# A hybrid attention and SSD layer: query and key rows permuted for their stores, decay rows in one load

## The chip, the cores and the metric

The kernel runs on one core of one Trainium2 chip. A core has TensorE (PE in the profile: matmuls; PEld: its weight loads), VectorE (DVE), ScalarE (ACT), GpSimd (POOL) and SyncE (SP), and 16 DMA engines that move data between its on-chip memory and DRAM. Nearly all transfers are issued by SP, one after the other. The metric is device time in microseconds, and a kernel is told by the median of its runs.

## The reference

One layer over 1024 tokens of width 2048. One input projection gives everything: queries (8 heads of 128), keys and values (2 heads), a gate, the queries and the key of a small indexer, and the inputs of an SSD (state space) mixer with 16 heads of 64.

- **Attention.** The indexer scores all keys of a query's own and earlier chunks of 64; each query keeps the best 256 and attends to these alone. Queries and keys are rotated by position in the first 32 of their 128 dimensions, where dimension i < 16 is paired with i + 16:

```python
x1 = t32[..., :half]
x2 = t32[..., half:rot]
out = jnp.concatenate([x1 * cos - x2 * sin, x2 * cos + x1 * sin, t32[..., rot:]], axis=-1)
```

- **SSD.** A causal convolution, then in chunks of 64 a masked product with decays exp(a_l - a_s), where a is the running sum of dt * A of each head, and a state that is carried from chunk to chunk.
- Both outputs are gated, multiplied by one output projection, added to the scaled input and normalised.

A score is a sum over the 128 dimensions of a head, so it is the same in whatever order queries and keys hold these dimensions, as long as it is one order for both.

## The kernel before

**Numbers.** A float32 factor is split into a rounded high part (ACT, `wh`, `xh`) and the rest (DVE or POOL, `wl`, `xl`), and each product is three matmuls. The projections use a seven-product scheme for pairs of tiles, with sums of inputs (`xf`), sums of weights (`ts`) and saved products (`p`, `u`) that go out to DRAM and come back.

**Tiling.** The tokens are two halves of 512. A tile of the input projection is 128 columns of its matrix by 512 tokens, with the columns on the partitions; which columns, `tile_cols` says. Results collect in four PSUM tiles `pj`; scores, transposes and SSD products use `a` and `o`.

**Queries and keys.** A query tile j of a group of four holds, for each of the four heads, dimensions 32j to 32j + 31. So tile 0 holds all that is rotated, and only there `rope_rows` runs: a shuffle of partitions inside groups of 32 (`SW16`), two products with tables (`rq`, `rk`) and a sum. A key tile holds 64 dimensions of both heads, and again tile 0 is the rotated one. Each tile is then stored to scratch in DRAM, `q_sc` (heads, 128 dimensions, 512 tokens) or `k_sc`, as 4 heads x 32 rows or 2 heads x 64 rows of 2 KB. There are 16 query stores and 4 key stores. Attention loads them again as 128 dimensions of a head (`t_kv`, `t_attn`) after all of a group are there.

**Decay rows.** `t_dt` stores the running sums of a half as 64 rows of 128 in `arow`. An SSD unit `t_ssd(h, g)` runs two rounds (`cp`) of two chunks; each round loads its 2 x 4 rows to all 128 partitions (`ar`), by one load for each chunk, and then takes ACT through two exponentials (`ea`), eight ReLUs with the column of each head and one wide exponential. There are 16 rounds.

**What sets the order.** The kernel's text is a planner. `Sim` holds a clock for each engine and estimated costs; tasks are generators that yield what they need; `Flow.pump` takes the first task by priority that is ready by these clocks, and every engine gets its instructions in the order in which they were emitted. PE's own work list is fixed, and other tasks are put between. A DMA is priced by

```python
        issue = 1000.0 if eng == "G" else 350.0
        row = max(sb.ap[-1][1] * 4, 64)
        self.clk["D"] = x + max(out.size(), in_.size()) * 4 * (1 / 360 + 0.6 / row)
```

where `row` is the last dimension of the tile on the chip's side, and takes one of eight lanes (semaphores), each of which is free again when its transfer has landed. On the chip each engine runs its list in order, and an instruction waits for the semaphores of what it uses. Nearly every instruction is recorded under line 312 in the profile (the planner's call), so instructions are told apart by their tiles.

Of the kernel before, what the change touches and what calls it, by code (L numbers as in the profile page):

```python
# [18 lines left out]
P = 128  # L19
# [18 lines left out]
O_Q, O_K, O_V, O_Z = 0, 1024, 1280, 1536  # L38
# [32 lines left out]
def xbc_col(g, j):  # L71
    return (256 * g + 128 * j) if j < 2 else (1024 + 128 * g if j == 2 else 1536 + 128 * g)


def tile_cols(kind, j):
    if kind == "misc":
        return [(O_KI, 64), (O_WI, 16), (O_DT, 16)]
    if kind == "q":
        return [(O_Q + 128 * (j // 4 * 4 + r) + 32 * (j % 4), 32) for r in range(4)]
    if kind == "k":  # L80
        return [(O_K + 128 * g + 64 * j, 64) for g in range(2)]
    base = {"qi": O_QI, "v": O_V, "z": O_Z}
    if kind in base:
        return [(base[kind] + 128 * j, 128)]
    g, i = j
    if kind == "zs":
        return [(O_ZS + 256 * g + 128 * i, 128)]
    return [(O_X + xbc_col(g, i), 128)]
# [494 lines left out]
class Layer:  # L583
# [774 lines left out]
    def rope_rows(self, h, x, name):  # L1358

        fl = self.fl  # L1360
        yield Need("", us=3)
        cos, sin, tmp = [fl.new("us", [P, HALF]) for _ in range(3)]
        fl.dma(cos, self.a[name][0, :, h * HALF:(h + 1) * HALF])
        fl.dma(sin, self.a[name][1, :, h * HALF:(h + 1) * HALF])
        yield Need("V")
        yield from self.rope(x, x, tmp, cos, sin, self.SW16)
        fl.free(cos, sin, tmp)

    def table(self, name, h):
# [5 lines left out]
            self.tab[name, h] = t  # L1375
        return self.tab[name, h]

    SW16 = [(i ^ 16) for i in range(32)]
    SW8 = [(i ^ 8) if i < 16 else i for i in range(32)]

    def rope(self, x, ps, tmp, cos, sin, perm):
# [263 lines left out]
    def s_k(self, h, j, x):  # L1645
        fl = self.fl
        if j == 0:
            yield from self.rope_rows(h, x, "rk")
        yield Need()
        fl.dma(self.k_sc[h].rearrange("(g p) s -> g p s", g=2)[:, 64 * j:64 * j + 64], x)  # L1650
        fl.free(x)
        fl.signal(self.ev_kv[h, j, "k"])

# [8 lines left out]
    def s_q(self, h, n, x):  # L1662
        fl = self.fl
        if n % 4 == 0:
            yield from self.rope_rows(h, x, "rq")
        yield Need()
        t = n % 4
        fl.dma(self.q_sc[h][n // 4][:, 32 * t:32 * t + 32], x)
        fl.free(x)
        fl.signal(self.ev_q[h, n])  # L1670

# [292 lines left out]
    def t_ssd(self, h, g):  # L1964
        fl, nc = self.fl, self.nc
# [7 lines left out]
        for cp in range(2):  # L1973
# [9 lines left out]
            ar = fl.new("s4", [P, 2, 4, P])  # L1983
            bn, xdt, xdd, hs, ea = [fl.new("u", [P, 2, 256]) for _ in range(5)]
            ea = ea.rearrange("p a (b l) -> p a b l", b=2)
            rows = self.arow[h].rearrange("(c n) l -> c n l", c=4)[2 * cp:2 * cp + 2, 4 * g:4 * g + 4, :]
            for k in range(2):
                fl.dma(ar[:, k], rows[k].partition_broadcast(P))
            for k, c in enumerate(cs):
                yield Need("P", late=2500.0, a=1)  # L1990
                b = fl.new("a", [P, 512])
# [18 lines left out]
            for q in range(2):  # L2010
                rq = slice(64 * q, 64 * q + 64)
# [39 lines left out]
            for j in range(2):  # L2051
                yield Need("P", now=True)
                for k, c in enumerate(cs):
                    for hh in range(2):
                        r = 2 * j + hh
# [248 lines left out]
        yield from self.ln_apply(0, st, dc)  # L2304


def rope_table(rot, dim, rows):
    half = rot // 2
    inv = (THETA ** (-np.arange(half) * 2.0 / rot)).astype(np.float32)
    ang = (np.arange(S, dtype=np.float32)[None, :] * inv[:, None]).astype(np.float64)  # L2310
    cos, sin = np.ones((rows, S)), np.zeros((rows, S))
    for p in range(rows):
        j = p % dim
        if j < rot:
            cos[p] = np.cos(ang[j % half])
            sin[p] = np.sin(ang[j % half]) * (-1.0 if j < half else 1.0)
    return np.stack([cos, sin]).astype(np.float32)


def layout(x, w_in, w_out, conv_w, conv_b, dt_bias, a_log, d_skip, ssd_norm_w, ln_g, ln_b):  # L2320
    xn = x[0]
    xt = np.ascontiguousarray(xn.T.reshape(KT // 2, 2, P, 2, HALF).transpose(3, 0, 2, 1, 4))
    wt = np.zeros((len(ORDER), D, P), np.float32)
    for t, (kind, j) in enumerate(ORDER):
        c0 = 0
        for off, n in tile_cols(kind, j):
            wt[t, :, c0:c0 + n] = w_in[0][:, off:off + n]
            c0 += n
    wt = np.ascontiguousarray(wt.reshape(len(ORDER), 2, 8, P, P).transpose(0, 1, 3, 2, 4)).reshape(len(ORDER), 2, P, 1024)
    wo = w_out[0].reshape(KT, P, 4, 512)[E_ORDER].reshape(8, 2, P, 4, 512)  # L2330
    wo = np.ascontiguousarray(wo.transpose(3, 0, 2, 1, 4)).reshape(4, 8, P, 1024)
    cw = np.zeros((P, 16, 5), np.float32)
    for g in range(4):
        for j in range(4):
            c = xbc_col(g, j)
            cw[:, 4 * g + j, 0:4] = conv_w[0][:, c:c + P].T
            cw[:, 4 * g + j, 4] = conv_b[0][c:c + P]
    dn = np.stack([np.repeat(d_skip[0], 64).reshape(8, P).T, ssd_norm_w[0].reshape(8, P).T], axis=1)
    hp = np.stack([dt_bias[0], a_log[0]])
    c3 = np.stack([np.eye(P), np.triu(np.ones((P, P))), np.ones((P, P))], axis=1).astype(np.float32)  # L2340
    return dict(xn=xn, xt=xt, wt=wt, wo=wo, cw=cw, dn=np.ascontiguousarray(dn), hp=hp, c3=c3, ri=rope_table(16, 64, P),
                rq=rope_table(32, 32, P), rk=rope_table(32, 64, P), lng=ln_g[0], lnb=ln_b[0])


# [12 lines left out]
```

## Time and profile before

| | |
|---|---|
| median of 3 runs | 1665.69 us (1662.65 to 1666.38) |
| span of the profiled execution | 1666.1 us, its own time, 0.4 above the median |
| instructions | 23979 |
| mean granted TensorE clock | 0.992 of full |
| DMA | 414.48 MB in 192387 packets, 249 GB/s, 71.7% of 16 engines on SP's queue |

A line of a view of groups gives the line, the engine, the operation, the written tile, an arrow and the tiles read, shapes and a count. In a timeline a line begins with its start and its length in us, and ends with the idle time of the engine ahead of it and what released it. Matmuls overlap: one of 512 columns is drawn as 0.39 us long, and the next begins 0.23 us after it. The table of windows has a line for each stretch: its length, the busy time of each engine, the granted clock (PEclk), the busy share of the DMA engines and what they moved.

### The profile page before, as it was taken

Reading aid. Unit: us, or ns where it says so; the run is one execution under the profiler, and the core shown is the slowest. Engines: PE = TensorE matmul, PEld = TensorE weight load, DVE = VectorE, ACT = ScalarE, POOL = GpSimd, SP = SyncE. Lnnn points to the kernel's source line nnn. Section 1 sums busy time; section 2 is a strip of 40 time slices with the busy share of each in tenths; the row PEclk is TensorE's granted clock in tenths of the full one; section 3 lists DMA queues with packets and bytes.
Section 4 is the critical chain, followed back from the end, with each engine's and each line's share of the span. In section 5 each row is a group of like instructions: output and inputs, shape, how many; then the busy total and the mean of one; then the engine's idle time right before and its main releaser. Section 6 shows DMA issues by size and latency. Waiting matters only on the chain. (4 is left out here: it accounts for less than half of the span.)

```text
span 1666.1 us, 23979 instructions
## 1 busy us (share of the span) xinstructions
PE 1620.1 (97%) x7996; PEld 1340.9 (80%) x7996; DVE 1321.7 (79%) x2429; ACT 1002.0 (60%) x1770; POOL 197.3 (12%) x215
## 2 busy tenths in 40 slices
PE   9999999999998989999999999999999999999997
PEld 7787777888787768888888888888877888888885
DVE  5889998997778866788676669875787687659998
ACT  4555666779787788776344456776866555532330
POOL 0100010000000000122212202222010000100110
PEclk9999999999999999999999999999999999999999
DMA  8177574789768856687786584656988889668664
GB/s 309 52 280 258 189 262 168 268 303 334 290 230 324 294 196 234 235 304 277 260 288 218 180 286 161 210 171 210 334 284 307 316 300 325 215 232 274 220 202 152
DMA packets 192387, 414.48 MB, mean 249 GB/s; under 512 B 19720, under 2 KB 55688, under 8 KB 192264
## 3 DMA queue, kind: packets, MB, share of 16 engines
q1 hardware_dynamic: 191832, 412.56, 71.7%
q8 instruction: 63, 1.03, 0.2%
q14 instruction: 60, 0.49, 0.1%
q10 hardware_dynamic: 432, 0.39, 0.1%
HBM read 308.94 MB, written 103.94 MB: 248 GB/s over the span
## 5 line engine op out<-in xcount | busy, mean ns | idle before, releaser
L312 PE MATMUL pj<-xh,wh 128*128 128x512 f32 (+1 forms) x1496 | 585.7, 392 | 14.5 <-ACT u L312 6.0
L312 PE MATMUL pj<-xh,wl 128*128 128x512 f32 (+1 forms) x1496 | 573.6, 383 | 5.1 <-DVE wl L312 5.1
L312 PE MATMUL pj<-xl,wh 128*128 128x512 f32 (+1 forms) x1496 | 573.0, 383 | 0.0
L312 DVE TENSOR_TENSOR wl<-wr,wh 128x1024 fp32r<-128x1024 f32 (+2 forms) x236 | 282.4, 1201 | 172.4 <-ACT wh L312 170.4
L312 PEld LDWEIGHTS pj<-xh,wh 128*128 128x128 f32 x1496 | 283.8, 190 | 68.6 <-issue 7.5
L312 PEld LDWEIGHTS pj<-xh,wl 128*128 128x128 f32 x1496 | 283.5, 190 | 63.1 <-DVE wl L312 7.3
L312 PEld LDWEIGHTS pj<-xl,wh 128*128 128x128 f32 x1496 | 284.0, 190 | 49.1
L312 ACT ACTIVATE wh<-wr 128x1024 fp32r<-128x1024 f32 (+2 forms) x242 | 248.1, 1031 | 120.0 <-PE pj L312 82.8
L312 PE MATMUL a<-u,u 128*128 128x512 f32 (+3 forms) x736 | 172.8, 354 | 7.6 <-DVE s L312 4.4
L312 PEld LDWEIGHTS a<-u,u 128*128 128x128 f32 x736 | 120.7, 189 | 42.5 <-DVE s L312 18.6
L312 ACT ACTIVATE u<-a 128x512 fp32r<-128x512 f32 (+4 forms) x115 | 53.2, 479 | 153.3 <-DVE u L312 58.0
L312 ACT ACTIVATE u<-s,sm 128x640 bf16<-128x640 int16 (+7 forms) x132 | 129.7, 983 | 22.1 <-DVE sm L312 20.0
L312 DVE TENSOR_TENSOR u<-u,u 128x512 f32<-128x512 f32 (+6 forms) x204 | 128.6, 645 | 5.7 <-DMA u<-wo 1.3
L312 PE MATMUL pj<-wh,xh 128*128 128x512 f32 x310 | 125.2, 404 | 0.5 <-DVE u L312 0.5
L312 PE MATMUL pj<-wh,xl 128*128 128x512 f32 x310 | 121.0, 390 | 0.0
L312 PE MATMUL pj<-wl,xh 128*128 128x512 f32 x310 | 121.0, 390 | 0.0
L312 ACT ACTIVATE a<-a 128x512 f32<-128x512 f32 (+3 forms) x160 | 77.1, 505 | 68.3 <-PE a L312 65.5
L312 ACT ACTIVATE u<-u 128x512 f32<-128x512 f32 (+4 forms) x146 | 80.1, 558 | 52.4 <-DVE u L312 43.9
L312 DVE TENSOR_TENSOR u<-pj,u 128x512 f32<-128x512 f32 (+2 forms) x112 | 74.7, 668 | 45.7 <-PE pj L312 42.2
L312 DVE TENSOR_TENSOR wr<-wr,wr 128x1024 f32<-128x1024 f32 (+1 forms) x81 | 99.8, 1233 | 0.8 <-DMA wr<-wt 0.4
L312 POOL TENSOR_SCALAR s<-s,sm 128x640 f32<-128x640 f32 (+7 forms) x64 | 63.8, 1011 | 124.0 <-DVE sm L312 97.4
L312 DVE SCALAR_TENSOR_TENSOR u<-cv,cw,u 128x512 f32<-128x512 f32 x96 | 73.0, 766 | 6.7 <-ACT u L312 3.5
(259 smaller groups left out, 2200.3 us busy)
## 6 DMA issues: line engine op xcount, KB each, us to landing
wr<-wt SPq DMA_DIRECT2D x187, 512.0 KB
u<-u SPq DMA_DIRECT2D x110, 256.0 KB
wr<-t SPq DMA_DIRECT2D x44, 512.0 KB
u<-wo SPq DMA_DIRECT2D x64, 256.0 KB
ts<-u SPq DMA_DIRECT2D x64, 256.0 KB
wr<-ts SPq DMA_DIRECT2D x32, 512.0 KB
s<-xt SPq DMA_DIRECT2D x24, 512.0 KB
t<-wr SPq DMA_DIRECT2D x22, 512.0 KB
```

The source lines that it names most:

```text
L312: f(*args, **kw)
```

## The change

The 128 dimensions of a head get a new order, `head_dim`. Row 4i + t of a query head is held in tile t at place i, so the four tiles of a group take every fourth row; a key tile takes every second. Rows 0, 4, 8 ... (tile 0) are still the 32 rotated dimensions, now with the pairs i and i + 16 next to each other, so that the shuffle swaps neighbours (`SW1` for queries; for keys, where the same rows lie two apart, `SW2`). The columns of the matrix are laid out on the host in that order, and the tables too. A tile's 4 heads x 32 rows are then rows t, t + 4, t + 8 ... of a scratch of 512 rows: one dimension of 128 rows, 8 KB apart (4 KB for keys). The bytes, the row length of 2 KB, the shuffles, products and loads stay as they are.

Each round of an SSD unit loads its decay rows by one DMA of 128 x 2 x 512 floats in place of two of 128 x 4 x 128.

```diff
+def head_dim(row):
+    i, t = divmod(row, 4)
+    return 32 * t + i if t else i // 2 + 16 * (i % 2)
+
 def tile_cols(kind, j):
...
     if kind == "q":
-        return [(O_Q + 128 * (j // 4 * 4 + r) + 32 * (j % 4), 32) for r in range(4)]
+        return [(O_Q + 128 * (j // 4 * 4 + r) + head_dim(4 * i + j % 4), 1) for r in range(4) for i in range(32)]
     if kind == "k":
-        return [(O_K + 128 * g + 64 * j, 64) for g in range(2)]
+        return [(O_K + 128 * g + head_dim(2 * i + j), 1) for g in range(2) for i in range(64)]
...
-        yield from self.rope(x, x, tmp, cos, sin, self.SW16)
+        yield from self.rope(x, x, tmp, cos, sin, self.SW1 if name == "rq" else self.SW2)
...
-    SW16 = [(i ^ 16) for i in range(32)]
+    SW1 = [(i ^ 1) for i in range(32)]
+    SW2 = [(i ^ 2) for i in range(32)]
...
-        fl.dma(self.k_sc[h].rearrange("(g p) s -> g p s", g=2)[:, 64 * j:64 * j + 64], x)
+        fl.dma(self.k_sc[h].rearrange("(m j) s -> j m s", j=2)[j], x)
...
-        fl.dma(self.q_sc[h][n // 4][:, 32 * t:32 * t + 32], x)
+        fl.dma(self.q_sc[h][n // 4].rearrange("r p s -> (r p) s").rearrange("(m t) s -> t m s", t=4)[t], x)
...
-            rows = self.arow[h].rearrange("(c n) l -> c n l", c=4)[2 * cp:2 * cp + 2, 4 * g:4 * g + 4, :]
-            for k in range(2):
-                fl.dma(ar[:, k], rows[k].partition_broadcast(P))
+            rows = self.arow[h].rearrange("(c n) l -> c (n l)", c=4)[2 * cp:2 * cp + 2, 4 * g * P:(4 * g + 4) * P]
+            fl.dma(ar.rearrange("p k n l -> p k (n l)"), rows.partition_broadcast(P))
...
-                rq=rope_table(32, 32, P), rk=rope_table(32, 64, P), lng=ln_g[0], lnb=ln_b[0])
+                rq=rope_table(32, [head_dim(4 * (p % 32)) for p in range(P)]),
+                rk=rope_table(32, [head_dim(2 * (p % 64)) for p in range(P)]), lng=ln_g[0], lnb=ln_b[0])
```

Since the planner prices a DMA by its size and rows, the order of the instructions is the same up to the first decay load and other from there on. On SP, the first round of the first SSD unit before (`s_953` takes the decay rows, `k_342` and `q_0` are scratch for keys and queries, `mask` the top-k masks, `u_0_7` a saved product):

```order
L312 DMA u_5493<-c_0_333 128x2x256
L312 DMA s_953_5496<-arow_283 128x512 x2
L312 DMA wr_5504<-t_0_7_4214 128x1024
L312 DMA wr_5505<-wt 128x1024
L312 DMA wr_5508<-wt 128x1024
L312 DMA k_342<-u_5262 2x64x512
...
L312 DMA wr_5643<-wt 128x1024
L312 DMA mask_329<-u_5651 128x640
L312 DMA q_0_287<-u_5372 4x32x512
L312 DMA q_0_287<-u_5547 4x32x512
L312 DMA u_5688<-u_0_7_4504 128x512
```

and in the changed kernel (the call is line 318 there):

```order
L318 DMA u_5493<-c_0_333 128x2x256
L318 DMA s_953_5496<-arow_283 128x2x512
L318 DMA wr_5503<-t_0_7_4214 128x1024
L318 DMA wr_5504<-wt 128x1024
L318 DMA wr_5507<-wt 128x1024
L318 DMA k_342<-u_5262 128x512
...
L318 DMA wr_5628<-wt 128x1024
L318 DMA wr_5663<-wt 128x1024
L318 DMA u_5672<-u_0_7_4504 128x512
L318 DMA q_0_287<-u_5372 128x512
L318 DMA q_0_287<-u_5546 128x512
L318 DMA mask_329<-u_5697 128x640
```

The two decay loads are one, the stores have one outer dimension of 128, and twenty rows later the load of the saved product and a weight load have moved ahead of the query stores and the mask behind them.

On ACT, the same round's exponentials before (`u_2976` and `u_3785` are top-k counts, `wh` high parts of weights; `pj_6006` and `pj_6057` are the two PSUM tiles of a pair of products, each of which is copied out once between its two parts and once after the second):

```order
L312 ACTIVATE u_6044<-pj_6006 128x512
L312 ACTIVATE u_2976,sm_2975<-s_109_745,sm_2975 128x896
L312 ACTIVATE u_2976,sm_2975<-s_110_746,sm_2975 128x1024
L312 ACTIVATE wh_6053<-wr_5787 128x1024
L312 ACTIVATE u_3785,sm_3784<-u_2425,sm_3784 128x384
L312 ACTIVATE u_3785,sm_3784<-u_2426,sm_3784 128x512
L312 ACT_TABLE_LOAD
L312 ACTIVATE u_5501<-s_953_5496 64x512 x2
L312 ACTIVATE s_953_5496<-s_953_5496,ac_241 128x128 x8
L312 ACTIVATE u_6107<-pj_6057 128x512
L312 ACTIVATE wh_6110<-wr_5856 128x1024
```

and in the changed kernel (the pair is `pj_5995` and `pj_6042` there):

```order
L318 ACTIVATE u_6083<-pj_6042 128x512
L318 ACTIVATE u_2976,sm_2975<-s_109_745,sm_2975 128x896
L318 ACTIVATE u_2976,sm_2975<-s_110_746,sm_2975 128x1024
L318 ACTIVATE wh_6092<-wr_5839 128x1024
L318 ACTIVATE u_3785,sm_3784<-u_2425,sm_3784 128x384
L318 ACTIVATE u_3785,sm_3784<-u_2426,sm_3784 128x512
L318 ACT_TABLE_LOAD
L318 ACTIVATE u_5501<-s_953_5496 64x512 x2
L318 ACTIVATE s_953_5496<-s_953_5496,ac_241 128x128 x8
L318 ACTIVATE cv_6149<-pj_5995 128x512
L318 ACTIVATE wh_6154<-wr_5868 128x1024
```

The block of exponentials has moved by half a round: before, the first copy of the second tile of the pair (`u_6107`) stands behind it; now that copy (`u_6083`) stands ahead of the counts, and the second copy of the first tile follows the block.

More of the change, by code (lines that the diff above doesn't have):

```diff
@@ L2304, in t_ln_b, with rope_table @@
         yield from self.ln_apply(0, st, dc)
-def rope_table(rot, dim, rows):
-    half = rot // 2
+def rope_table(rot, dims):
+    half, rows = rot // 2, len(dims)
     inv = (THETA ** (-np.arange(half) * 2.0 / rot)).astype(np.float32)
@@ L2312, in rope_table @@
     for p in range(rows):
-        j = p % dim
+        j = dims[p]
         if j < rot:
@@ L2340, in layout @@
     c3 = np.stack([np.eye(P), np.triu(np.ones((P, P))), np.ones((P, P))], axis=1).astype(np.float32)
-    return dict(xn=xn, xt=xt, wt=wt, wo=wo, cw=cw, dn=np.ascontiguousarray(dn), hp=hp, c3=c3, ri=rope_table(16, 64, P),
-                rq=rope_table(32, 32, P), rk=rope_table(32, 64, P), lng=ln_g[0], lnb=ln_b[0])
+    return dict(xn=xn, xt=xt, wt=wt, wo=wo, cw=cw, dn=np.ascontiguousarray(dn), hp=hp, c3=c3, ri=rope_table(16, [p % 64 for p in range(P)]),
+                rq=rope_table(32, [head_dim(4 * (p % 32)) for p in range(P)]),
+                rk=rope_table(32, [head_dim(2 * (p % 64)) for p in range(P)]), lng=ln_g[0], lnb=ln_b[0])
 def kernel(**inputs):
```

## The prediction

> **What bounds the kernel now.** I read the page first, then the table of windows, then the waits of TensorE and of SP's queue, and last the timelines around the long waits.
>
> ```profile
> PE 1620.1 (97%) x7996; PEld 1340.9 (80%) x7996; DVE 1321.7 (79%) x2429; ACT 1002.0 (60%) x1770; POOL 197.3 (12%) x215
> ```
>
> TensorE (PE) is busy for 97% of the span, and the change takes no matmul away. All it can win lies in PE's gaps, in stretches of low granted clock and in the ends. The windows, cut at the stages (us, PE busy, weight loads, DVE, ACT, POOL, granted clock, DMA share, GB/s), say where PE's gaps are:
>
> ```profile
> 160.00:300.00 140.00, 132.73 (x681) 107.20 (x681) 126.96 (x215) 88.26 (x152) 8.94 (x8) 0.98 0.59 205
> 440.00:545.00 105.00, 98.38 (x431) 80.49 (x430) 80.26 (x178) 84.59 (x156) 6.25 (x9) 0.98 0.76 272
> 545.00:620.00 75.00, 68.96 (x305) 55.95 (x304) 57.20 (x125) 58.67 (x111) 1.68 (x5) 0.98 0.70 246
> 620.00:1655.00 1035.00, 1026.42 (x5234) 858.32 (x5232) 803.92 (x1456) 569.78 (x991) 160.07 (x162) 1.00 0.73 249
> 1655.00:1667.00 12.00, 0.00 (x0) 0.00 (x0) 7.30 (x13) 0.00 (x0) 0.98 (x1) 0.66 0.46 149
> ```
>
> Not busy: 7.3 us in 160-300, 6.6 in 440-545, 6.0 in 545-620, and only 8.6 in the 1035 us after that. The last 12 us are the final layer norm, whose instructions the change leaves in the same order. So 20 us of gaps lie in the three stages in which queries and keys are stored, and the rest of the program is nearly full.
>
> **The stores.** The tile view of the stores gives what one costs SP to issue (ns, least, median, most):
>
> ```profile
> L312 SPq DMA_DIRECT2D q<-u x16: 511/522/912, 208.4 to 571.3; - x16
> L312 SPq DMA_DIRECT2D k<-u x4: 516/524/613, 168.9 to 548.4; - x4
> L312 SPq DMA_DIRECT2D c<-u x32: 319/323/681, 340.5 to 1274.8; - x32
> ```
>
> A store of the same 256 KB with 128 rows outside (c) issues in 323 ns, a query store with 4 outside in 522. Twenty stores save 20 x 0.2 = 4 us of SP. What else they cost shows behind them in the queue. Timeline lines (start, length, engine, operation; in brackets idle time and its releaser) of SP, DVE, ACT, PE and POOL:
>
> ```profile
> 281.45 0.55 SPq L312 DMA_DIRECT2D q<-u  x1
> 282.55 0.42 SPq L312 DMA_DIRECT2D s<-xt  x1
> 291.19 1.22 DVE L312 TENSOR_TENSOR s<-s,xr 128x1024 f32<-128x1024 f32 x1 [2.91 <-DMA s<-xt]
> 292.33 2.35 DVE L312 TENSOR_TENSOR wl<-wr,wh 128x1024 fp32r<-128x1024 f32 x2
> 289.41 1.04 ACT L312 ACTIVATE wh<-wr 128x1024 fp32r<-128x1024 f32 x1
> 290.50 0.39 PE L312 MATMUL pj<-xh,wh 128*128 128x256 f32 x1 [1.34 <-ACT wh L312]
> 293.61 0.58 PE L312 MATMUL pj<-xh,wl 128*128 128x256 f32 x1 [2.60 <-DVE wl L312]
> ...
> 208.38 2.00 SPq L312 DMA_DIRECT2D q<-u  x2
> 221.81 0.42 SPq L312 DMA_DIRECT2D s<-xt  x1
> 228.09 2.52 POOL L312 TENSOR_TENSOR s<-s,xr 128x1024 f32<-128x1024 f32 x1 [26.50 <-DMA ts<-u]
> ```
>
> The load of x at 282.55, 1.1 us behind a query store, is used at 291.19: 8.64 us, and DVE had waited 2.91 us for it. The same load at 221.81, 12 us after the last such stores, was used 6.28 us later at the latest. [...]
>
> Where this reaches PE, stage by stage:
>
> At 291: the sum on DVE would start 2.3 us earlier (282.55 + 6.28 = 288.83) and end at 290.05. The split of weights behind it, 2.35 us for two, waits for ACT's half, which is there by 290.45, and its first half ends near 291.7. PE then goes on at 291.7 in place of 293.61: **-1.9 us** (bounds 0 and -2.6, its whole idle time).
>
> At 571: a load of a saved product is issued 0.6 us behind a query store, and used 10.7 us later.
>
> ```profile
> 560.69 0.48 SPq L312 DMA_DIRECT2D u<-u  x1
> 571.37 0.69 DVE L312 TENSOR_TENSOR cv<-pj,u 128x512 f32<-128x512 f32 x1 [2.49 <-DMA u<-u]
> 573.10 0.28 ACT L312 ACTIVATE u<-a 128x128 f32<-128x128 f32 x1 [5.59 <-DVE u L312]
> 585.10 0.57 ACT L312 ACTIVATE u<-pj 128x512 f32<-128x512 f32 x1
> 585.73 0.50 PE L312 MATMUL pj<-xh,wh 128*128 128x512 f32 x1 [1.74 <-ACT u L312]
> ```
>
> DVE waits 2.49 us, ACT behind it 5.59, and from 573.10 ACT works without a pause to the copy at 585.10, for which PE idles 1.74. With the load in time the whole run is about 2.5 us earlier and the gap closes: **-1.7 us** (bounds 0, if the new order fills that time, and -1.7).
>
> At 519 PE's longest gap stands at the end of a run of ACT and DVE that begins before it:
>
> ```profile
> 481.82 2.02 DVE L312 TENSOR_TENSOR u<-u,u 128x512 f32<-128x512 f32 x3 [1.14 <-DMA u<-rq]
> 484.23 0.83 ACT L312 ACTIVATE u<-s,sm 128x640 bf16<-128x640 f32 x1 [0.88 <-DVE sm L312]
> 519.37 0.77 PE L312 MATMUL pj<-xh,wh 128*128 128x512 f32 x1 [4.89 <-DVE u L312]
> ```
>
> Most of those 4.89 us are the top-k counts on ACT, which no DMA delays. A late rotation table costs DVE 1.14 us at 481.82, and ACT then waits 0.88 for DVE. That much can pass down the run: **-0.9 us** (bounds 0 and -1.14).
>
> **The granted clock.** It falls to half behind some gaps:
>
> ```profile
> 293.50:297.00 3.50, 3.39 (x16) 3.40 (x17) 3.46 (x8) 0.00 (x0) 0.00 (x0) 0.52 0.89 317
> 585.70:589.20 3.50, 3.47 (x15) 2.90 (x16) 3.50 (x5) 1.35 (x2) 0.00 (x0) 1.00 0.62 238
> 618.50:622.00 3.50, 3.44 (x8) 2.79 (x9) 1.56 (x2) 3.47 (x7) 0.30 (x2) 0.50 0.65 211
> 622.00:625.50 3.50, 3.50 (x11) 2.77 (x11) 2.64 (x4) 3.30 (x7) 0.00 (x0) 0.63 0.63 210
> ```
>
> After PE's 2.60 us gap the clock is 0.52 for 3.5 us, a loss of 3.5 x 0.48 = 1.7 us; after the 1.74 us gap it stays 1.00. What is left at 291 (0.7 us, right behind the 1.34 at 290.50) may or may not still trip it: I take half, **-0.85 us** (bounds 0 and -1.7). [...]
>
> **The decay rows.** One load replaces two, 16 times:
>
> ```profile
> L312 SPq DMA_DIRECT2D s<-arow x32: 332/430/681, 544.6 to 1428.0; - x32
> SPq L312 <- DMA q<-u: 9.4, 5, 2.2
> SPq L312 <- DMA s<-arow: 4.9, 7, 1.1
> ```
>
> SP issues 16 x 0.43 = 6.9 us less. With the stores' 4 us, and up to 14.3 us in which SP itself waited for a query store or a decay load to land, SP gets freer; but in the waits of PE, DVE and ACT no row names an arow load, and both loads of a pair are used together. I cost it at nothing, covered by the matmuls; were that cover gone, one load less ahead of a weight load is worth 0.43 us.
>
> **The new order.** The planner prices the one load below the two, so from the first SSD unit (545 us) every later choice shifts. This is most of what the change does by count of instructions, and it cuts both ways. One place can be read. Before, the exponent block of the decay rows (table load, two exponentials, eight ReLUs) stands on ACT directly ahead of a copy out of PSUM for which PE waits:
>
> ```profile
> 612.98 1.28 ACT L312 ACT_TABLE_LOAD   x1
> 614.28 1.28 ACT L312 ACTIVATE u<-s 64x512 f32<-64x512 f32 x2
> 615.58 2.44 ACT L312 ACTIVATE s<-s,ac 128x128 f32<-128x128 f32 x8
> 617.93 0.57 ACT L312 ACTIVATE u<-pj 128x512 f32<-128x512 f32 x1
> 618.56 0.80 PE L312 MATMUL pj<-xh,wh 128*128 128x512 f32 x1 [4.31 <-ACT u L312]
> ```
>
> 5.0 us of ACT there leave PE idle for 4.31, and the two windows after 618.50 (clock 0.50, 0.63) lose 3.5 x 0.50 + 3.5 x 0.37 = 3.1 more: 7.4 us together. In the changed order that copy (the saved product, u_6083) stands one round ahead of the block; behind it come a copy that frees a tile needed later and weights first needed after 24 more matmuls. So this gap should go: **-7.4 us** (bounds 0 and -7.4). But the other decay blocks, evacuations and splits fall elsewhere too. After 620 only 8.6 us of gaps are left to lose, while the three windows before it lost 20 in 320 us, so a new draw is likelier worse than better there. Between 0 and one new gap of the same kind (+7.4) I take the middle, **+4 us**.
>
> Sum: -1.9 - 1.7 - 0.9 - 0.85 - 7.4 + 4 = -8.75 us. The profiled span is 1666.1, 0.4 above the median of 1665.69, so 1657.35 by span and **1657 us** as a median.
>
> [...]
>
> **Rivals.** (a) A gap comes back: the stores help, but one more decay block or late split falls ahead of something PE needs, at +7.4: 1657 + 7.4 = 1664.4, within the noise. For it: there are 16 such blocks of 5 us, and ACT is busy for 58.67 of the 75 us before 620. Against it: 15 of the 16 cost PE nothing like that so far. Chance 0.22. (b) Slower: the new order places decay blocks ahead of PSUM copies at several more places just after 620, where the counts still fill ACT. Kept gains are 5.4 us (the first four terms), so from two blocks net it is slower: 1665.7 - 5.4 + 2 x 7.4 = 1675. For it: one such block did cost 7.4. Against: ACT is busy only 569.78 of 1035 us after 620. Chance 0.15. (c) The change doesn't do what it says: stores with 128 outer rows, 8 KB apart in memory, land as late as before. Only the order's terms stay, -3.4: 1662. Against it: c, of the same size, issues in 323 ns and nobody waits for it. Chance 0.05. The forecast has 0.58.
>
> **Range and chances.** Two in ten may lie outside. The forecast's own spread is its unknown terms: the new order at 0 (-4), the two bounds left of the clock and of the gap at 291 (-1.6), and a second such place emptied, some 2 us: 1649. Upward it reaches through (a), at 1664.4, and half a block beyond: 1669. The likeliest case alone has 1650 to 1662. A measurement of this kernel tells about 0.2%, 3.3 us, from no change. Faster than 1662.4: the forecast, half of (c): 0.60. Within: most of (a), the rest of (c): 0.24. Slower than 1669.0: (b) and a little of (a): 0.16.
>
> **What would show it.** Query and key stores issue in about 0.32 us and SP waits for none of them. DVE's 2.91 us wait near 288 is gone and PE's gap near 291 is under 1 us, with 160-300 about 2 us fuller; up to there the order is the same, so this is the cleanest sign. No DVE wait of over 1 us for a load stands between 440 and 620. PE's gap behind the first decay block is gone, and the clock near 618 is full. After 620 PE is idle for 8 to 16 us. The prediction is wrong if the waits for loads stay, which is (c), or if windows after 620 hold far more than 16 us of gaps, which is (b).

## The result, and the profile after

The changed kernel takes 1686.80 us (median of 4 runs, 1684.35 to 1687.99) against 1666.04 for the kernel before on the same chip: a ratio of 1.0130, 95% interval 1.0114 to 1.0145. It is 21 us slower. The prediction was 1657 us, 9 faster; 1686.8 lies outside its range of 1649 to 1669.

The page of the changed kernel still has PE busy for 97%, with the same 7996 matmuls, and a longer span of 1686.0 us:

```profile
PE 1627.5 (97%) x7996; PEld 1346.7 (80%) x7996; DVE 1325.5 (79%) x2430; ACT 993.4 (59%) x1764; POOL 205.2 (12%) x219
```

The windows at the stages, with the long last stretch cut in two (us, busy time of PE, weight loads, DVE, ACT, POOL, granted clock, DMA share, GB/s), first after:

```profile
160.00:300.00 140.00, 134.57 (x707) 108.98 (x707) 127.84 (x219) 92.32 (x160) 9.55 (x8) 0.99 0.59 210
545.00:620.00 75.00, 74.06 (x332) 60.54 (x330) 55.97 (x123) 57.86 (x107) 4.82 (x10) 1.00 0.76 268
620.00:1000.00 380.00, 373.84 (x1962) 314.67 (x1961) 273.95 (x552) 218.63 (x394) 83.12 (x65) 1.00 0.73 249
1000.00:1300.00 300.00, 282.38 (x1422) 236.99 (x1421) 230.72 (x414) 192.62 (x349) 49.06 (x70) 0.96 0.69 232
```

and the two later ones of the kernel before:

```profile
620.00:1000.00 380.00, 377.71 (x1984) 319.75 (x1982) 275.48 (x556) 220.87 (x406) 71.03 (x59) 0.99 0.74 253
1000.00:1300.00 300.00, 294.98 (x1518) 246.05 (x1517) 238.82 (x431) 211.88 (x366) 57.36 (x77) 0.99 0.73 242
```

Up to 620 us the kernel is better filled, as forecast: PE gains 1.8 us in 160-300 and 5.1 in 545-620. Then 620-1000 loses 3.9 us of busy time and 1000-1300 loses 12.6, and the clock of the latter falls from 0.99 to 0.96, some 9 us more of 300. PE idles 23.8 us in these two stretches alone, where the prediction had 8 to 16 for all that follows 620.

The stores do what was said. The tile view of the changed kernel (ns, least, median, most) has

```profile
L318 SPq DMA_DIRECT2D q<-u x16: 319/320/382, 207.4 to 562.4; - x16
L318 SPq DMA_DIRECT2D k<-u x4: 319/323/728, 167.9 to 543.9; - x4
```

and in its waits SP stands 0.6 us for query stores where it was 9.4:

```profile
SPq L318 <- DMA q<-u: 0.6, 2, 0.3
```

The timeline around the sum of x shows DVE working straight through it, with no wait for the load, and PE's 2.60 us gap down to 0.76:

```profile
279.53 0.32 SPq L318 DMA_DIRECT2D q<-u  x1
280.38 0.49 SPq L318 DMA_DIRECT2D s<-xt  x1
286.26 1.22 DVE L318 TENSOR_TENSOR s<-s,xr 128x1024 f32<-128x1024 f32 x1
289.83 0.39 PE L318 MATMUL pj<-xh,wl 128*128 128x256 f32 x1 [0.76 <-DVE wl L318]
```

The loss stands elsewhere. PE's longest new gap ends at 1210.62 (the expectations below name a gap by where it begins, here 1204, and have 6.8 us for it where the row has 6.37). The timeline ahead of it, on ACT, DVE and PE of the changed kernel:

```profile
1191.77 1.28 ACT L318 ACT_TABLE_LOAD   x1
1193.06 1.28 ACT L318 ACTIVATE u<-s 64x512 f32<-64x512 f32 x2
1194.37 2.45 ACT L318 ACTIVATE s<-s,ac 128x128 f32<-128x128 f32 x8
1196.84 1.28 ACT L318 ACT_TABLE_LOAD   x1
1198.14 0.63 ACT L318 ACTIVATE u<-u 128x512 f32<-128x512 f32 x1
1198.67 1.04 ACT L318 ACTIVATE wh<-wr 128x1024 fp32r<-128x1024 f32 x1
1199.75 1.23 DVE L318 TENSOR_TENSOR wl<-wr,wh 128x1024 fp32r<-128x1024 f32 x1 [6.29 <-ACT wh L318]
1209.79 0.68 DVE L318 TENSOR_TENSOR u<-pj,u 128x512 f32<-128x512 f32 x1
1210.62 0.77 PE L318 MATMUL pj<-xh,wh 128*128 128x512 f32 x1 [6.37 <-DVE u L318]
```

and the windows behind it:

```profile
1210.00:1213.40 3.40, 2.79 (x7) 2.24 (x8) 3.40 (x5) 0.66 (x2) 0.00 (x0) 0.50 0.71 232
1213.40:1216.80 3.40, 3.40 (x11) 2.69 (x10) 2.23 (x5) 0.60 (x1) 0.00 (x0) 0.61 0.81 314
```

Read the timeline from below: PE waits 6.37 us for DVE's sum at 1209.79, which frees a PSUM tile. DVE is busy from 1199.75 to there with splits and sums, and had idled 6.29 us ahead of them because the first split's other half `wh` came late on ACT. ACT was in a block of decay rows with a table load on either side, 6.3 us together. Then PE runs for two windows at about half clock. The timeline has the same chain at 1278, with one link more: the copy on ACT for which PE waits 5.04 us had itself waited for DVE:

```profile
1281.52 1.23 DVE L318 TENSOR_TENSOR wl<-wr,wh 128x1024 fp32r<-128x1024 f32 x1 [7.94 <-ACT wh L318]
1283.50 0.28 ACT L318 ACTIVATE u<-a 128x128 f32<-128x128 f32 x1 [2.02 <-DVE u L318]
1283.83 1.22 PE L318 MATMUL a<-u 128*128 128x128 f32 x4 [5.04 <-ACT u L318]
```

### The profile page after: what moved, and what is told of

The parts are those of the page before. It is cut to its first block, busy times and chain, and to the rows that moved or that the text cites. A ratio compares the mean times of both kernels' runs of the same rounds, so it can differ in the third digit from the quotient of the medians.

```text
span 1686.0 us, 23971 instructions
## 1 busy us (share of the span) xinstructions
PE 1627.5 (97%) x7996; PEld 1346.7 (80%) x7996; DVE 1325.5 (79%) x2430; ACT 993.4 (59%) x1764; POOL 205.2 (12%) x219
## 5 line engine op out<-in xcount | busy, mean ns | idle before, releaser
L318 DVE TENSOR_TENSOR u<-u,u 128x512 f32<-128x512 f32 (+6 forms) x212 | 137.1, 659 | 7.3 <-DMA u<-zs 2.6
L318 DVE TENSOR_TENSOR wr<-wr,wr 128x1024 f32<-128x1024 f32 (+1 forms) x75 | 92.4, 1233 | 1.3 <-DMA wr<-wt 0.8
L318 POOL TENSOR_SCALAR s<-s,sm 128x640 f32<-128x640 f32 (+7 forms) x64 | 59.7, 949 | 165.1 <-DVE sm L318 126.0
```

What stands on the lines that cost most here:

```text
L318: f(*args, **kw)
```

## The experiments

Since the planner emits the program, what the chip does and what the planner is told can be had apart: the real DMAs are issued, and the planner's clocks are advanced for others.

### Order or transfers: four kernels

The permuted stores with the two old loads (`e1_stores_only`); the one load with the old stores (`e2_load_only`); both new transfers in the old order (`e3_old_order`); both old transfers in the new order (`e4_new_order`). The last two by

```diff
+    def dma_told(self, real, told):
+        for out, in_ in real:
+            self.nc.sync.engine.dma_start(out, in_)
+        for out, in_ in told:
+            self.placed(self.sim.run("SP", "dma_start", [out], [in_], {}))
...
-            fl.dma(ar.rearrange("p k n l -> p k (n l)"), rows.partition_broadcast(P))
+            fl.dma_told(one, two)     # e4: fl.dma_told(two, one)
```

> The permuted stores alone, decay rows in two loads: every engine's list is that of the kernel before, entry by entry, and only the twenty stores have another shape. Theory O (the loss is the new order behind the first decay load): the four terms of the stores are kept, so 1666 - 5.4 = about 1660.5 us (1658 to 1663), and the half-clock window near 618 is still there. Rival S (the strided stores themselves cost later transfers time): at least 1680.

> One decay load, stores as before: every engine's list is that of the changed kernel. Theory O: slower than the changed kernel by what the stores gave, 1686.8 + 5.4 = about 1692 us (1686 to 1696). Rival S (stores guilty): 1666 or less. Rival L (the one larger load, by itself, is late or crowds others): about 1692 as well, and the next two kernels tell O from L.

> Both transfers of the change on the chip, while the planner is told of the old two decay loads: the lists are those of the kernel before, with one decay load in place of each pair. Theory O: as with the stores alone, 1660.5 us, within 2 us of it, since the loads themselves were costed at nothing. Rival L: 1680 or more. If fewer entries on the queue of SP do help, 1 to 4 us below the stores alone.

> Neither transfer of the change, but its order: two decay loads on the chip and the old stores, while the planner is told of one load. Theory O: about 1692 us (1686 to 1698), as with the one load and the old stores. Rivals S and L: 1666, as before, since no transfer is changed.

| | old order | new order |
|---|---|---|
| old stores, two loads | 1665.11 (before) | 1691.36 (e4), 1.0164 [1.0145, 1.0183] |
| old stores, one load | | 1688.07 (e2), 1.0144 [1.0124, 1.0164] |
| new stores, two loads | 1659.74 (e1), 0.9969 [0.9956, 0.9982] | |
| new stores, one load | 1660.12 (e3), 0.9965 [0.9952, 0.9978] | 1686.80 (the change), 1.0130 [1.0114, 1.0145] |

All four times lie in the ranges of theory O. The order alone costs 26 to 27 us in either full row; the stores give 5.4 us in the old order, and 1.3 by medians in the new one, which can't be told from nothing there; the single load gives nothing that can be told in either. The stores alone leave every list as it was: it is the decay load, which gains nothing, that brings the new order. The windows of 1000-1300 go with the order, not with the transfers: the old order with both new transfers, and then the new order with neither,

```profile
1000.00:1300.00 300.00, 296.15 (x1531) 247.13 (x1529) 238.41 (x429) 210.69 (x362) 57.38 (x77) 1.00 0.74 244
```

```profile
1000.00:1300.00 300.00, 281.73 (x1427) 236.16 (x1426) 230.02 (x418) 192.28 (x349) 49.04 (x70) 0.97 0.69 231
```

### The two blocks, taken away one at a time

In the new order most of one round's decay work on ACT is left out: the eight ReLUs and two table loads go, and the exponentials become copies or get scale 0. Everything else is issued as it was. First it is the round at 1193 (`e5_bare_round`), then the one at 1274 (`e6_bare_later`).

```diff
+            bare, fl.rounds = fl.rounds in BARE, fl.rounds + 1     # BARE = (6,), then (7,)
...
-                    fl.act(ar[:, k, r], ar[:, k, r], AF.Relu, bias=col, scale=-1.0)
+                    if bare:
+                        fl.act_told(ar[:, k, r], ar[:, k, r], AF.Relu, bias=col, scale=-1.0)   # planner only
...
```

> The changed kernel and its order, entry by entry, but for one of the 16 decay rounds (the seventh, on ACT from 1191.8 to 1198.1 us) most of its work on ACT is left out: the eight ReLUs are not issued, the two narrow exponentials are copies and the wide one has scale 0, so that two table loads go as well. This part of the result is not the reference's. 5.0 us of ACT go ahead of the weight split for which DVE idled 6.29 us and behind which the copy stands that frees PE's tile. Theory B (this block makes the gap of 6.8 us at 1204): gap under 2 us and no half-clock window behind it, 1686.8 - 5.0 - 3.4 = about 1678 us (1676 to 1681). Rival C (a tile or a transfer makes the gap): unchanged, 1685 or more. Rival D (the gaps at 1244 and 1278 are only the echo of this one): they go too, about 1665.

> The same for the round after it (on ACT from 1273.0 to 1279.4 us), and for that one alone; what is left out is the same. Theory B: the gap of 5.4 us at 1278 falls to under 1 us, and the half-clock window behind it goes: 1686.8 - 5.0 - 3.4 = about 1678 us; the gap at 1204 stays. Rival C: unchanged, 1685 or more. Rival D: unchanged as well, since an echo comes from the earlier gap.

1678.79 us (1.0085 [1.0061, 1.0109]) and 1678.27 (1.0084 [1.0065, 1.0102]): 8.0 and 8.5 us less than the change, as theory B had it. In the first, DVE's idle time and PE's gap shrink (timeline), and the clock behind stays full (window):

```profile
1193.64 1.23 DVE L321 TENSOR_TENSOR wl<-wr,wh 128x1024 fp32r<-128x1024 f32 x1 [1.32 <-ACT wh L321]
1204.51 0.47 PE L321 MATMUL pj<-xh,wh 128*128 128x512 f32 x1 [1.40 <-DVE u L321]
```

```profile
1204.50:1208.00 3.50, 3.49 (x15) 2.91 (x16) 3.47 (x6) 2.11 (x3) 0.00 (x0) 1.00 0.98 286
```

In the second, the gap at 1278 is 0.27:

```profile
1277.79 0.71 PE L321 MATMUL a<-u 128*128 128x128 f32 x4 [0.27 <-ACT u L321]
```

Each left the other gap where it was, so neither is the echo of the other (rival D falls).

### The same two blocks, only moved

Nothing is left out in `e10_two_held`: ACT's ten entries of each of the two rounds are issued later, and the planner isn't told.

```diff
+HOLD = {6: 13, 7: 6}        # round: entries of ACT to wait for
...
+        if eng == "A" and self.taken is not None:
+            self.taken.append(real)
+            return
         real()
+        if eng == "A" and self.behind:
+            self.behind[0] -= 1
+            if not self.behind[0]:
+                for r in self.behind[1]:
+                    r()
+                self.behind = None
...
```

> The changed kernel and its order, nothing left out; on ACT the ten entries of the seventh decay round are issued 13 entries later (behind the wide exponential of the round before and a weight split), those of the eighth 6 entries later (directly ahead of the next round's). Both then share a table load. Theory B (place, not work, makes the gaps at 1204 and 1278): both gaps under 2 us, 1686.8 - 8.0 - 8.5 = about 1670 us (1667 to 1674). Rival W (it is the work: ACT simply has 5 us too many there): the gaps move behind the new places, 1680 or more.

1669.60 us, 1.0032 [1.0020, 1.0045]: 17 us less, at the expected number. ACT does the same exponentials 12 us later, behind the splits and behind another round's wide exponential, so that no table load of its own stands ahead of them, and DVE waits 1.32 us where it waited 6.29. At the second place PE goes on without a gap (last line):

```profile
1194.16 1.04 ACT L404 ACTIVATE wh<-wr 128x1024 fp32r<-128x1024 f32 x1
1195.24 1.23 DVE L404 TENSOR_TENSOR wl<-wr,wh 128x1024 fp32r<-128x1024 f32 x1 [1.32 <-ACT wh L404]
1202.47 1.06 ACT L404 ACTIVATE s<-s 128x1024 f32<-128x1024 f32 x1
1205.54 1.27 ACT L409 ACTIVATE u<-s 64x512 f32<-64x512 f32 x2
1206.11 0.47 PE L404 MATMUL pj<-xh,wh 128*128 128x512 f32 x1 [1.41 <-DVE u L404]
1270.92 0.60 PE L404 MATMUL a<-u 128*128 128x128 f32 x4
```

So it was the place of these blocks: every exponential and ReLU of theirs is still done. The place had a price in work too, since each block needed table loads of its own there: ACT loads a table 47 times in the changed kernel and 43 times in this one, at 1.28 us each. How much of the 17 us these four loads are was not told apart. Two of sixteen blocks account for 17 of the order's 27 us.

### A gap behind POOL, removed and given back

At 1244 of the changed kernel PE waits 2.8 us for a power of two columns that stands on POOL behind a weight split. `e11_pool_swapped` is `e10_two_held` with that pair swapped.

```diff
+        if eng == "G" and outs[0].tensor.name == "wl_2300_12490":
+            self.late = real          # issued behind the next entry of POOL
+            return
...
```

> The kernel with the two rounds held, and on POOL one pair of entries swapped: the power of the gate (128x2) ahead of the weight split of 2.67 us behind which it stood at 1246.84 and for which PE waited 2.78. Theory: that gap goes, and the half-clock windows behind it (3.4 or 6.8 us long): 2.8 + 1.7 to 3.4 = 4.5 to 6.2 us less than with the two rounds held, about 1665 us. Rival: DVE, which waits 3.02 us for a copy that stands behind that split on POOL, is what PE waits for next: at most 1.5 us less.

1671.99 us, 1.0044 [1.0029, 1.0060], which can't be told from the 1.0032 without the swap: the theory missed, and the rival, under which at most 1.5 us go, fits. The timelines, without the swap and then with it:

```profile
1239.82 0.68 POOL L404 TENSOR_TENSOR sm<-sm,mhalf 128x2 f32<-128x2 f32 x1
1240.56 1.22 PE L404 MATMUL a<-c,sm 128*128 128x128 f32 x4 [2.79 <-POOL sm L404]
1240.67 2.33 DVE L404 SCALAR_TENSOR_TENSOR u<-cv,cw,u 128x512 f32<-128x512 f32 x3 [3.01 <-POOL cv L404]
1260.92 0.61 PE L404 MATMUL a<-o,u 128*128 128x1 f32 x4 [0.97 <-DVE u L404]
```

```profile
1237.75 2.20 POOL L407 TENSOR_TENSOR sm<-sm,mhalf 128x2 f32<-128x2 f32 x1 [61.93 <-DVE sm L407]
1240.01 0.71 PE L407 MATMUL a<-c,sm 128*128 128x128 f32 x4 [0.49 <-POOL sm L407]
1242.47 2.33 DVE L407 SCALAR_TENSOR_TENSOR u<-cv,cw,u 128x512 f32<-128x512 f32 x3 [3.06 <-POOL cv L407]
1260.85 0.61 PE L407 MATMUL a<-o,u 128*128 128x1 f32 x4 [2.95 <-DVE u L407]
```

PE gains 2.3 us at 1240, but DVE still waits 3 us for the copy behind the split on POOL, and PE's next wait for DVE, 20 us on, grows from 0.97 to 2.95.

### The one gap that the new order did remove

`e9_old_order_held` is the old order with both new transfers, and the first decay round held back by two entries of ACT, behind the PSUM copy that the prediction named.

```diff
+HOLD = {0: 2}
```

> The order before with both transfers of the change; of its lists only ACT's is edited, at one place: the ten entries of the first decay round (two exponentials, eight ReLUs) are issued two entries later, behind the copy out of PSUM and the weight split that stood behind them. Nothing is left out. The prediction's term for this place: the gap of 4.2 us near 608 and the two half-clock windows behind it go, -7.4: 1660.1 - 7.4 = 1652.7 us (1650 to 1655). Rival: the gap only moves, to the counts that now stand behind the block, and the time stays within 2 us of 1660.

1655.54 us, 0.9950 [0.9935, 0.9965], the fastest kernel of the study: by medians 4.6 us below the old order without the hold, though the intervals of the two (0.9965 [0.9952, 0.9978]) overlap. (The two profiled executions are only 2.3 us apart.) The profile says where a part of the 7.4 went. The windows without the hold, and then with it:

```profile
545.00:620.00 75.00, 71.10 (x308) 58.06 (x308) 57.95 (x124) 61.10 (x114) 1.98 (x7) 0.95 0.70 251
620.00:1000.00 380.00, 376.15 (x1989) 318.63 (x1988) 280.45 (x561) 220.31 (x403) 68.48 (x57) 1.00 0.75 254
```

```profile
545.00:620.00 75.00, 75.00 (x338) 61.82 (x337) 57.84 (x125) 61.21 (x115) 1.98 (x7) 1.00 0.70 252
620.00:1000.00 380.00, 373.73 (x1974) 315.88 (x1973) 282.64 (x565) 222.65 (x409) 70.44 (x57) 1.00 0.76 256
```

In 545-620 it gains the whole term, 3.9 us of PE and 0.05 x 75 = 3.75 of clock (3.4 to 4.1, since the clock is rounded). Then 2.4 come back behind it, where PE now waits for a copy on ACT:

```profile
627.94 0.50 PE L404 MATMUL pj<-xh,wh 128*128 128x512 f32 x1 [1.44 <-ACT u L404]
```

### Three other orders

The changed kernel, with both its transfers, was planned anew by telling the planner of shorter runs for the decay rows, and of nothing else.

```diff
-        row = max(sb.ap[-1][1] * 4, 64)
+        row = max(min(sb.ap[-1][1] * 4, CAP if "arow" in in_.tensor.name else 4096), 64)   # CAP = 1400, 640, 400
```

> The changed kernel, with both its transfers, whose planner is told of decay rows in runs of 1400 B in place of 2048: one load costs 0.07 us more in the plan, and the order is another from about 950 us on. Theory P (the loss lies in places like the one at 1204, and that one stands in the plan itself: between the planner's own clocks PE idles 5.8 us there; in this order the plan has no gap over 2.8 us behind 545 us, and ends 2.3 us earlier): 1660 to 1670 us. Rival R (every order drawn anew behind the first decay load loses about 20 us by what the plan does not know): 1680 or more.

> As the one before, with runs of 640 B told: 0.34 us more for one load in the plan. The order on ACT is that of the kernel before for some two thirds of its list, and another behind that; the plan has one gap of 2.1 us and ends 0.6 us later than that of the kernel before. Theory P: 1658 to 1666 us. Rival R: 1675 or more, less than 1680 since part of the order is the old one.

> Once more the changed kernel with both its transfers, its planner told of runs of 400 B: 0.79 us more for one load than for runs of 1400 B, and a third order that is another from the first decay round on. The plan has no gap over 1.7 us behind 545 us and ends 2.0 us later than that of the kernel before. Theory P (what is lost can be read from the plan's own gaps): 1660.1 + 2.0 = 1662 us, at most 1665. Theory M, after the two kernels with 1400 and 640 B (the chip loses 8 to 14 us to an order drawn anew beyond what its plan shows, since the old order's places have been tried on the chip and the new one's have not): 1670 to 1676 us.

(The step in price from 1400 to 400 B is 0.56 us; 0.79 is the whole term of the latter.)

| order | end of its plan, against the old order's | measured (ratio) | against the old order with the same transfers, 1660.1 |
|---|---|---|---|
| the change (2048 B) | +4.1 us | 1686.80 (1.0130) | +26.7 |
| 1400 B | +1.8 | 1673.81 (1.0051 [1.0031, 1.0072]) | +13.7 |
| 640 B | +0.6 | 1670.19 (1.0028 [1.0015, 1.0041]) | +10.1 |
| 400 B | +2.0 | 1667.18 (1.0009 [0.9999, 1.0019]) | +7.1 |

Theories P, R and M all missed, each by 2 to 6 us from the near end of its range. The plan's own end puts the worst order last but doesn't rank the other three; each order loses 5 to 23 us beyond it, and all four stay 7 to 27 us behind the old one. The plan of the change does hold the gap at 1204: on the planner's own clocks PE stands still for nearly 6 us there. Of the gap at 1278 it has nothing. The end of the plan and that gap come from the planner alone, so they could have been read without a run.

## Why the prediction was wrong

**Stores: right.** "At 291", "at 571", "at 519" and the clock sum to -5.4 us; the stores alone measured -5.4. That both are 5.4 is partly luck, as the places show. PE's gap at 291 shrank by 1.8 where -1.9 was said. That a load behind a store with 128 outer rows comes in time was the author's estimate; the runs show it (8.64 us from its issue to its use before, 5.88 in the changed kernel, where DVE doesn't wait for it), and not why. The gap at 585 is gone, and in the new order with the old stores a gap of the same kind is there again (2.2 us, ending at 589.5). The clock term, half a chance of 1.7, was a chance: the changed kernel has a half-clock stretch of 3.41 us at 291 (granted clock 0.99 over 160-300), the stores alone have none (1.00). The term at 519 wasn't seen: that gap was 4.2 to 6.0 us from kernel to kernel with one order up to there, a spread larger than the 0.9 said. The traces' semaphore updates tell the two shapes apart: a query store of the kernel before left 5 updates when it landed and a key store 3, and in the changed kernel each leaves 16, as the c stores do in both. What these numbers count no run shows.

**Decay rows at nothing: right** for the load itself. One load or two made no difference that can be told, in either order.

**The gap behind the first decay block, -7.4: right in place and size, too large as a gain.** It measured 7.65 us in 545-620 and some 5 after the next wait took its part. The sum should have named what is late next.

**"The new order", +4: this step failed.** Its bounds were 0 and 7.4, one new gap of the same kind. With the first block's gap gone, the new order nets +26.7, so this term was between +32 and +34 (26.7 and the 5 to 7.65 of that gap). The mechanism was in the text: a decay block on ACT ahead of something that PE waits for, 7.4 us each; two such blocks cost 8.0 and 8.5. That is rival (b), and its price of a block holds. But it counted two blocks net, 1675 us, where two came and one went; about half of the term lies elsewhere, and its cause stays open. And it placed the blocks "just after 620, where the counts still fill ACT", and they came at 1193 and 1274. The argument against it, ACT's 569.78 busy us of 1035, was the error: an engine that is idle for 45% of a stretch still makes everything wait that stands behind a 6.3 us run on its list. What stood behind was not a copy, as at 618, but a weight split, and through it the head of DVE's list.

The bounds were also read from the wrong rows. "15 of the 16 cost PE nothing like that so far" is true of the old order, and says nothing of sixteen new places. And "a new draw is likelier worse than better" was given 4 us where four draws cost 7 to 27.

**What stays open.** Beyond the two blocks, the new order still loses about 10 us net (1669.6 against 1660.1). Its profile has new gaps of 1.2 to 2.9 us that begin at 667, 1013, 1244, 1355 and 1432, with half clock behind four of them. Only the one at 1244 was tried, and its removal gave nothing. Why the old order is better than all four new ones wasn't tested.

## What to carry to other kernels

Where a program is placed by costs, a cheaper instruction is two changes: the instruction, and a new order for everything behind it. Measure them apart, by issuing the one and telling the planner the other; here the transfers were worth -5 us, all of it from the stores, which leave the order alone; the order was worth +27, and the decay load that brought it gained nothing. The old order with the new transfers and one block held back (1655.5 us) beats both kernels. When you bound what a new order can cost, count the long runs of an in-order engine and ask what stands directly behind each in the new lists, on the engine that reads its result too; the mean load of that engine doesn't bound it.

## What the hardware showed beside

**One gap of PE was followed by half clock, another as long by full clock.** The stores alone and the old order with both transfers reach the same place with the same gap of PE. The gap in the timeline and the window behind it, in the first and then in the second:

```profile
1271.41 0.64 PE L318 MATMUL a<-o,u 128*128 128x1 f32 x4 [1.48 <-DVE u L318]
```

```profile
1271.90:1275.20 3.30, 3.30 (x10) 2.72 (x11) 1.95 (x5) 2.49 (x5) 0.00 (x0) 0.50 1.03 346
```

```profile
1273.57 0.61 PE L318 MATMUL a<-o,u 128*128 128x1 f32 x4 [1.47 <-DVE u L318]
```

```profile
1274.00:1277.40 3.40, 3.40 (x19) 2.90 (x19) 2.05 (x5) 2.53 (x5) 0.00 (x0) 1.00 1.06 410
```

After 1.48 us the clock is half for 3.3 us, after 1.47 it is full. A gap of 1.5 us is thus worth 1.5 or, by an estimate of half of 3.4 us more, 3.2 us. The clock records of the kernel before and of the changed one say more. In them a half-clock stretch ahead of the last matmuls lasts 3.41 or 6.83 us, and all begin at whole steps of 3.413 us from the first: 18, 84, 113 and 307 steps behind it in the kernel before, and 65, 111, 213, 269, 280, 290 and 335 in the changed one. Cut into such steps from 100 to 1640 us, all 11 in which PE idled 1.9 us or more were followed by half clock, and 4 of the 7 with 1.45 to 1.89 us. What tells the two gaps above apart isn't shown.

**Two columns on POOL took 2.20 us.** In the rows of the swap above, the same 128x2 power took 0.68 us behind the split and 2.20 directly beside DVE's work (a sum of two tiles that DVE ran from 1238.19 to 1239.41). It is seen from the other side as well: in the changed kernel a 128x256 product on DVE that elsewhere takes 0.42 us takes 2.64 beside a sum on POOL (why either is long isn't shown):

```profile
1265.88 2.39 POOL L318 TENSOR_TENSOR wr<-wr,wr 128x1024 f32<-128x1024 f32 x1 [8.45 <-DMA wr<-wt]
1265.91 2.64 DVE L318 TENSOR_TENSOR u<-u 128x256 f32<-128x256 f32 x1
```
